# A transformer layer's W_out and W_up stages: splits held to the end of the DFT, products begun in parts, combinations spread over steps

## The chip, the core and the metric

The kernel runs on one core of a Trainium2 chip. Its engines work side by side, each with its own instruction queue that is taken in order: TensorE (PE in the profile; PEld is its weight load) multiplies matrices into PSUM banks, VectorE (DVE), ScalarE (ACT) and GpSimd (POOL) work element by element, SyncE (SP) issues most DMAs. An instruction that waits for data holds up everything behind it in its own queue. The metric is device microseconds of one execution; the time of a kernel is the median of its runs.

## What is computed

One layer of a bidirectional encoder and a last norm, for two groups of tokens with shared weights: the "sample" (512 tokens) and the "prompt" (1024 tokens), with 16 meta tokens ahead of each. All data is float32, D is 1024, the hidden width 4096.

```python
def encoder_layer(x, w_in, rel_bias, meta_bias, w_branch_na, w_branch_fn, w_out, g_mix, g_mlp, w_up, w_down):
    h = rmsnorm(x, g_mix)
    z = h @ w_in
    q, k, v, u, gate_na, gate_fn = jnp.split(
...
    y_na = neighbourhood_attention(q, k, v, rel_bias, meta_bias).reshape(B, N, NA_WIDTH) @ w_branch_na
    y_fn = fourier_mix(u) @ w_branch_fn
    mixed = jax.nn.sigmoid(gate_na) * y_na + jax.nn.sigmoid(gate_fn) * y_fn
    x = x + mixed @ w_out
    a = jax.nn.relu(rmsnorm(x, g_mlp) @ w_up)
    return x + (a * a) @ w_down
```

`fourier_mix` is the real part of a 2-D DFT over positions and channels.

## The kernel before

**Float32 by splits.** A product of float32 matrices is made of three fast ones: each operand is split into a rounded part `hi` and a rest `lo`, and `mm3` issues hi·hi, hi·lo and lo·hi into one PSUM bank. For a weight tile a DMA on SP loads `w_raw` (L145), ScalarE casts it to `w_hi` (L151), and GpSimd subtracts to get `w_lo` (L152). The buffers `w_raw`, `w_hi` and `w_lo` of `wtile` exist twice each; tiles can be given other places.

**The order.** The sample goes through all stages first, then the prompt. In each: attention, gates, the merge of the attention branch, the Fourier stage (`fourier_channels` for the channels, split into `uc` and `us` at L132 and L133; `fourier_positions`, the DFT over positions, which leaves `fs` and splits it into `fT` at L982 to L997), `merge_fn` (W_fn, eight tiles `dm`), `project_out` (W_out), W_up, W_down. The program is written in this order, but the framework's scheduler orders each engine's queue by its own estimate of when operands are ready, so an instruction written later can stand ahead of one written earlier. Two helpers bound that freedom: `behind(marks)` puts what is issued inside it behind the marked instructions in the queues of the engines that the marks belong to (it adds no wait for them to end), and `pinned()` does so with the last instruction written so far on every engine, TensorE included.

**W_out's weights** are eight pieces of 256 rows by 512 columns; the generator `out_weights` makes one load and split per `next(wout)`. `merge_fn` asks for one after every second tile, so four in all (L891); the other four are asked for after it. The pieces' places differ: in the sample, the first lies in the MLP pool's `w` pair, four in `wo` pairs, one in `wu`, one in the `hi`/`lo` buffers of `wtile`, the last in the `w` pair again.

**The merge.** In `merge_fn` VectorE multiplies each product with its gate (L884) and adds the attention branch (L885); for each pair of tiles ScalarE casts the sum (L889) and VectorE subtracts (L890). The result `m` has four parts, each of them two of the eight blocks that W_out's products sum over. During the sample's Fourier stage VectorE also combines W_fn's columns for both groups (`fn_ahead`, L801 to L809).

**W_out's products.** For the sample (`Layer.project_out`) a half of the columns at a time, for four tiles of 128 tokens, each a bank of 24 products, added to the residual `acc` (L1025). In the second half each token tile is then normed, transposed on TensorE (L193) and split into `h2T`, two tiles behind. Then the first two W_up tiles begin with the first 256 tokens (`up`, step 256; L1065 to L1070), and the last two transposes stand between. `Mlp.run` then goes on with these tiles' second half, and with the next tiles in steps of 512; after every second pair come the products with W_down (`down`).

For the prompt (`Halves.project_out`) the order of token tiles and halves is written out by hand in `steps`, with two kinds of banks in turn, and `flush` puts transposes where they are due.

**W_up for the prompt** (`Halves.up`) works in sixteen groups `g` of two tiles. It is a Strassen-like scheme: seven products of twelve matmuls each instead of eight, from combined weights that `prepare` makes for the next group (GpSimd at L1305, ScalarE at L1308), one step of it behind each product. VectorE adds the products (L1416, L1423, L1426), the relu's squares follow (L1433), and four combinations of them (L1439) are made for the W_down stage, in two tiles `h0` and `h1` that are stored by DMA (L1441).

Of the kernel before, what the change touches and what calls it, by code (L numbers as in the profile page):

```python
# [22 lines left out]
ALU = mybir.AluOpType  # L23
# [45 lines left out]
class Layer:  # L69
# [783 lines left out]
    def merge_fn(self, br, mp, T, fT, mixed, sig, gate, wout, marks):  # L853

        nc = self.nc
        m = []
        ready, self.fn_ready = self.fn_ready, []
        got, banks = {}, {}
# [14 lines left out]
        for dm in range(8):  # L873
            if dm % 2 == 0:
                total = []
            total.append(mp.tile([128, D], F32, name="hn", bufs=2)[:, :T])
            sg, mx = (t[dm // 2][:, dm % 2] for t in (sig, mixed))
            for c in range(T // 512):
                cs = slice(c * 512, (c + 1) * 512)
                if (dm, c) in banks:  # L880
                    py = product(dm, c, self.LAST[-1:], banks[dm, c], more=True)
                else:
                    py = product(dm, c, self.LAST, self.psum())
                nc.vector.tensor_tensor(out=sg[:, cs], in0=py, in1=sg[:, cs], op=ALU.mult)  # L884
                nc.vector.tensor_tensor(out=total[-1][:, cs], in0=mx[:, cs], in1=sg[:, cs], op=ALU.add)  # L885
            if dm % 2:
                m.append((gate(), gate()))
                for i in range(2):
                    nc.scalar.copy(out=m[-1][0][:, i], in_=total[i])  # L889
                    nc.vector.tensor_tensor(out=m[-1][1][:, i], in0=total[i], in1=m[-1][0][:, i].bitcast(F32), op=ALU.subtract)  # L890
                self.wo.append(next(wout))  # L891
        return m
# [65 lines left out]
    def fourier_positions(self, q, fp, name, T, u, cos, sin):  # L958
        nc = self.nc
# [7 lines left out]
        for m in self.LAST:  # L967
            fs = q.tile([128, K], F32, name="fs", bufs=2)
            for k0, kn in kchunks:
                ps = self.psum()  # L970
                ops = []
# [22 lines left out]
            else:  # L994
# [3 lines left out]
                                               op0=ALU.mult, op1=ALU.subtract)  # L998
        return fT, marks

# [7 lines left out]
    def project_out(self, hp, p, x, T, m, wo, acc, mlp, marks):  # L1008
# [5 lines left out]
        for t in range(nt):  # L1014
            nc.sync.dma_start(acc[t], x[t * 128:(t + 1) * 128, :])
        pending = []
        for half in range(2):
            cs = slice(half * 512, (half + 1) * 512)
            w = wo[4 * half:4 * half + 4]
            for t in range(nt):  # L1020
                ts = slice(t * 128, (t + 1) * 128)
# [119 lines left out]
class Halves:  # L1141
# [55 lines left out]
    def project_out(self, hp, mp, m, wo):  # L1197
# [12 lines left out]
        def flush(n):  # L1210
            with layer.behind(layer.mark((mybir.EngineType.PE,))):
                for x in due.pop(n, ()):
                    self.turn(*x)

        def product(n, t, half):
# [3 lines left out]
            ps = layer.psum(("mm", "o")[n % 2])  # L1219
            layer.mm3(ps, [(m[kt // 2][0][:, kt % 2, ts], m[kt // 2][1][:, kt % 2, ts], w[kt // 2][0][:, kt % 2], w[kt // 2][1][:, kt % 2])  # L1220
                           for kt in range(8)])
            nc.vector.tensor_tensor(out=acc[t][:, cs], in0=acc[t][:, cs], in1=ps, op=ALU.add)
# [169 lines left out]
    def up(self, mp):  # L1392

        layer, nc, TH = self.layer, self.nc, self.TH
        for g in range(self.NF // 2):
            steps = self.prepare(g + 1)

            def step():
                with layer.pinned():
                    next(steps, None)  # L1400

# [30 lines left out]
            for i, x in enumerate((r, r_)):  # L1432
                nc.vector.tensor_tensor(out=x, in0=x, in1=x, op=ALU.mult)  # L1433
                nc.sync.dma_start(to[:, i * 2 * TH:(i + 1) * 2 * TH], x)
            h = [self.tile(f"h{i}") for i in range(2)]
            s1, s2, s3, s4 = (x[:, y] for x in h for y in (left, right))
            for k, x, y, op in ((s1, r[:, right], r_[:, right], ALU.add), (s2, s1, r[:, left], ALU.subtract),
                                (s3, r[:, left], r[:, right], ALU.subtract), (s4, r_[:, left], s2, ALU.subtract)):
                nc.vector.tensor_tensor(out=k, in0=x, in1=y, op=op)  # L1439
# [205 lines left out]
```

## Time and profile before

| | us |
|---|---|
| median of 3 runs | 2032.23 |
| lowest, highest | 2029.92, 2033.35 |
| the profiled execution | 2034.05 |
| its span, first to last instruction | 2032.3 |

The page of the profile counts, for each engine, the busy time, its share of the span and the instructions. A row of the timeline has the start in us from the span's start, the duration, the engine, the line of the kernel, the operation, output<-inputs and shapes; in brackets stands how long the engine was idle before it and what released it. A row that ends in x2 or more holds several instructions in a row. In the table by stretch, each engine's busy time and number of instructions come first, in the order PE, PEld, DVE, ACT, POOL, then the granted TensorE clock as a share of full speed, the DMA engines' busy share and GB/s.

### The profile page before, as it was taken

How to read it: one execution, taken by the hardware profiler on the slowest of the kernel's cores; microseconds unless marked ns; L12 is line 12 of the kernel's file. 1: busy time of each engine (PE TensorE's matmuls, PEld its weight loads, DVE VectorE, ACT ScalarE, POOL GpSimd, SP SyncE). 2: the span in 40 equal slices, each digit the busy share in tenths (PEclk: the TensorE clock that was granted, in tenths of full speed). 3: DMA queues.
4: the chain of work that ended last, by engine and by line, in shares of the span. 5: the costliest groups of instructions: out<-in, count | busy, mean ns of one | idle time of the engine just before them, and what ended most of it. 6: DMA issues, size and time to landing. Idle time of an engine off the chain costs nothing.

```text
span 2032.3 us, 26413 instructions
## 1 busy us (share of the span) xinstructions
PE 1955.3 (96%) x9611; PEld 1622.2 (80%) x9611; DVE 1138.2 (56%) x1914; ACT 756.4 (37%) x1323; POOL 961.9 (47%) x743
## 2 busy tenths in 40 slices
PE   6999979999999989999999999999999999999997
PEld 4887767888888878888888888787787888888886
DVE  6672434666665552566663226566767776442246
ACT  3564322433333221556552313124333333533342
POOL 3244535366777641233333226113788785544442
PEclk9999989999999999999999999999999999999999
DMA  6666772344444445455455544222445445976663
GB/s 204 170 160 213 213 219 83 121 138 158 155 145 154 148 149 207 116 140 139 136 179 167 142 111 146 99 72 77 169 150 196 157 154 180 312 238 201 196 190 122
DMA packets 275652, 326.50 MB, mean 161 GB/s; under 512 B 42872, under 2 KB 197240, under 8 KB 274968
## 3 DMA queue, kind: packets, MB, share of 16 engines
q1 hardware_dynamic: 261792, 303.92, 46.9%
q0 software_dynamic: 13728, 20.88, 4.4%
q8 instruction: 76, 1.25, 0.3%
q14 instruction: 56, 0.46, 0.1%
HBM read 235.67 MB, written 91.64 MB: 161 GB/s over the span
## 4 chain that ended last, share of the span: by engine, by line
PE 77%; DVE 7%; DMA 5%; issue 4%; POOL 4%; ACT 3%; SPq 0%; POOLq 0%; DVEq 0%; ACTq 0%
PE ps_mm L128 22%; PE ps_o L128 20%; PE ps_s L128 17%; PE ps_t L128 7%; PE ps_mm L487 2%; PE ps_mm L488 2%; PE ps_mm L489 2%; PE ps_o L629 1%; POOL w_lo L152 1%; DVE hn L885 1%; PE ps_t L609 1%; DVE gate L890 1%; DMA w_raw<-in_w_in 1%; DMA gain<-in_w_fnB 1%; DMA w_raw<-in_w_out 1%
## 5 line engine op out<-in xcount | busy, mean ns | idle before, releaser
L152 POOL TENSOR_TENSOR w_lo<-w_raw,w_hi 128x1024 fp32r<-128x1024 f32 x84 | 212.4, 2537 | 228.1 <-ACT w_hi L151 202.8
L151 ACT CAST w_hi<-w_raw 128x1024 fp32r<-128x1024 f32 x100 | 104.8, 1049 | 168.5 <-PE ps_mm L128 49.9
L1068 DVE TENSOR_TENSOR relu<-relu 128x512 f32<-128x512 f32 (+1 forms) x34 | 65.6, 1929 | 109.2 <-ACT relu L1067 109.0
L487 PE MATMUL ps_mm<-hT,w_hi 128*128 128x512 f32 (+3 forms) x320 | 125.9, 393 | 0.0
L488 PE MATMUL ps_mm<-hT,w_hi 128*128 128x512 f32 (+3 forms) x320 | 114.8, 359 | 0.0
L489 PE MATMUL ps_mm<-hT,w_lo 128*128 128x512 f32 (+3 forms) x320 | 114.7, 358 | 0.0
L1305 POOL TENSOR_TENSOR x<-w_hi,x 128x512 fp32r<-128x512 f32 (+1 forms) x42 | 78.6, 1872 | 22.8 <-ACT x L1308 22.8
L603 ACT ACTIVATE sc<-sc,ast 128x288 f32<-128x288 f32 (+4 forms) x96 | 53.9, 562 | 78.4 <-DVE ast L601 78.0
L152 POOL TENSOR_TENSOR w_lo<-r,w_hi 128x1024 fp32r<-128x1024 f32 x15 | 35.9, 2395 | 96.7 <-ACT w_hi L151 96.7
L723 POOL MEMSET bm<- 64x96 f32 (+2 forms) x64 | 11.2, 176 | 144.3 <-DVE ast L601 105.5
L629 PEld LDWEIGHTS ps_o<-pt,vb 104*64 104x64 f32 (+6 forms) x576 | 61.7, 162 | 11.7 <-POOL vb L566 5.0
L152 POOL TENSOR_TENSOR w_lo<-w_hi 128x1024 fp32r<-128x1024 f32 x18 | 47.1, 2615 | 48.7 <-ACT w_hi L151 48.7
L128 PE MATMUL ps_t<-gate,x 128*128 128x512 f32 x264 | 65.5, 397 | 2.7 <-DVE r_lo L1416 2.7
L152 POOL TENSOR_TENSOR w_lo<-w_lo,w_hi 128x1024 fp32r<-128x1024 f32 x18 | 45.9, 2551 | 45.6 <-ACT w_hi L151 45.6
L489 PEld LDWEIGHTS ps_mm<-hT,w_lo 128*128 128x128 f32 x320 | 60.1, 188 | 8.5
L629 PE MATMUL ps_o<-pt,vb 104*64 104x128 f32 (+6 forms) x576 | 62.8, 244 | 4.0 <-POOL vb L566 2.3
L566 POOL TENSOR_TENSOR vb<-vr,vb 96x384 fp32r<-96x384 f32 (+4 forms) x48 | 48.6, 1032 | 35.5 <-ACT vb L565 30.2
L128 PE MATMUL ps_mm<-gate,x 128*128 128x512 f32 x256 | 64.2, 395 | 0.0
L488 PEld LDWEIGHTS ps_mm<-hT,w_hi 128*128 128x128 f32 x320 | 60.7, 190 | 1.7
L487 PEld LDWEIGHTS ps_mm<-hT,w_hi 128*128 128x128 f32 x320 | 60.6, 189 | 1.7
L128 PEld LDWEIGHTS ps_t<-gate,x 128*128 128x128 f32 x264 | 48.7, 188 | 16.1 <-DVE r_lo L1416 5.1
L601 DVE CUSTOM_DVE_ANT_0 sc<-ps_s,bm 128x288 f32<-128x288 f32 (+4 forms) x96 | 46.3, 482 | 26.9 <-PE ps_s L597 10.9
(672 smaller groups left out, 5890.3 us busy)
## 6 DMA issues: line engine op xcount, KB each, us to landing
w_raw<-in_w_in SPq DMA_DIRECT2D x56, 512.0 KB
w_raw<-in_w_up SPq DMA_DIRECT2D x34, 512.0 KB
wt<-hn SPq DMA_DIRECT2D x32, 512.0 KB
hidden_prompt<-h SPq DMA_DIRECT2D x32, 512.0 KB
w_hi<-hidden_prompt SPq DMA_DIRECT2D x20, 512.0 KB
w_raw<-hidden_prompt SPq DMA_DIRECT2D x18, 512.0 KB
w_lo<-hidden_prompt SPq DMA_DIRECT2D x18, 512.0 KB
w_raw<-in_w_out SPq DMA_DIRECT2D x16, 512.0 KB
```

Source lines behind the costliest of these rows:

```text
L128: self.nc.tensor.matmul(out, a, b, start=(i == 0 and not more), stop=(i == len(terms) - 1), skip_group_check=more)
L151: nc.scalar.copy(out=hi, in_=raw)
L152: (lo_engine or nc.gpsimd).tensor_tensor(out=lo, in0=raw, in1=hi.bitcast(F32), op=ALU.subtract)
L487: nc.tensor.matmul(ps, a[0], b[0], start=(kt == 0), stop=False)
L488: nc.tensor.matmul(ps, a[0], b[1], start=False, stop=False)
L489: nc.tensor.matmul(ps, a[1], b[0], start=False, stop=(kt == 7))
L566: nc.gpsimd.tensor_tensor(out=lo, in0=vs, in1=hi.bitcast(F32), op=ALU.subtract)
L601: nc.vector.tensor_tensor_reduce(out=sc[:, :W], in0=ps[:, :W], in1=bm[:, :W], scale=1.0, scalar=3e38, op0=ALU.add, op1=ALU.min, accum_out= ...
L603: nc.scalar.activation(out=sc[:, :W], in_=sc[:, :W], func=AF.Exp, bias=st[:, 0:1], scale=-1.0, accum_out=st[:, 1:2])
L629: nc.tensor.matmul(po[:m, j * 128:(j + 1) * 128], v, x, start=(i == 0), stop=(i == len(ops) - 1))
L1068: nc.vector.tensor_tensor(out=r, in0=r, in1=r, op=ALU.mult)
L1305: self.nc.gpsimd.tensor_tensor(out=to, in0=x, in1=y, op=op)
```

## The change

It has five parts.

- `fourier_positions` also returns a mark of the last ScalarE and the last GpSimd instruction written in it, and `merge_fn` asks for its four W_out pieces behind these marks: the casts and subtractions of W_out may no longer be queued ahead of the DFT's own on these two engines. SP's queue is not marked.
- Sample, `project_out`: the first two banks get their products over the first six of eight blocks, one bank after the other, before either gets its last two blocks. The number of products is the same.
- Prompt, `Halves.project_out`: the same for its first two steps.
- Sample: the third W_up tile is loaded into the MLP pool's `w` pair instead of the `wtile` buffers, is worked in steps of 256 tokens, and its first half is issued ahead of `Mlp.run`.
- Prompt, `Halves.up`: the four combinations and their two stores leave the end of their group; a generator issues them one by one in the steps of the next group, behind its products. Those of the last group follow the loop.

```diff
     merge_fn
+        marks, split = marks
...
-                self.wo.append(next(wout))
+                with self.behind(split):
+                    self.wo.append(next(wout))
     fourier_positions
-        return fT, marks
+        return fT, (marks, self.mark((mybir.EngineType.Activation, mybir.EngineType.Pool)))
     project_out (sample)
+        def product(ps, half, t, blocks, more=False):
+            ts = slice(t * 128, (t + 1) * 128)
+            w = wo[4 * half:4 * half + 4]
+            self.mm3(ps, [(m[kt // 2][0][:, kt % 2, ts], m[kt // 2][1][:, kt % 2, ts], w[kt // 2][0][:, kt % 2], w[kt // 2][1][:, kt % 2])
+                          for kt in blocks], more=more)
+            return ps
+        banks = {(0, t): product(self.psum(), 0, t, range(6)) for t in range(2)}
         for half in range(2):
...
-                ps = self.psum()
-                self.mm3(ps, [(m[kt // 2][0][:, kt % 2, ts], m[kt // 2][1][:, kt % 2, ts], w[kt // 2][0][:, kt % 2], w[kt // 2][1][:, kt % 2])
-                              for kt in range(8)])
+                if (half, t) in banks:
+                    ps = product(banks[half, t], half, t, range(6, 8), True)
+                else:
+                    ps = product(self.psum(), half, t, range(8))
...
         mlp.load(1)
-        for f in range(2):
+        mlp.load(2, self.pair(p, [128, 2, 512], "w", 2))
+        for f in range(3):
             next(mlp.ups[f])
-            self.transpose_in(*pending.pop(0))
+            if pending:
+                self.transpose_in(*pending.pop(0))
     Mlp
-    def load(self, f):
+    def load(self, f, to=None):
         if f not in self.w:
-            self.w[f] = self.layer.weights(self.layer.rows("w_up", f * 128))
+            to = to and [x.rearrange("p a (k c) -> p (a k) c", c=128) for x in to]
+            self.w[f] = self.layer.weights(self.layer.rows("w_up", f * 128), to)
...
-            step = 256 if f < 2 and T == 512 else 512
+            step = 256 if f < 3 and T == 512 else 512
     Halves.project_out (prompt)
+            if n < 2 and n not in banks:
+                banks[n] = layer.psum(("mm", "o")[n % 2])
+                layer.mm3(banks[n], ops[:6])
+                return
+            ps = banks[n] if n < 2 else layer.psum(("mm", "o")[n % 2])
+            layer.mm3(ps, ops[6 if n < 2 else 0:], more=n < 2)
...
+        for n in range(2):
+            product(n, *steps[n])
     Halves.up (prompt)
+        combining = iter(())
...
                 with layer.pinned():
+                    next(combining, None)
                     next(steps, None)
...
-            h = [self.tile(f"h{i}") for i in range(2)]
-            s1, s2, s3, s4 = (x[:, y] for x in h for y in (left, right))
-            for k, x, y, op in ((s1, r[:, right], r_[:, right], ALU.add), (s2, s1, r[:, left], ALU.subtract),
-                                (s3, r[:, left], r[:, right], ALU.subtract), (s4, r_[:, left], s2, ALU.subtract)):
-                nc.vector.tensor_tensor(out=k, in0=x, in1=y, op=op)
-            for i, x in enumerate(h, 2):
-                nc.sync.dma_start(to[:, i * 2 * TH:(i + 1) * 2 * TH], x)
+            combining = self.combinations(r, r_, to)
+        for _ in combining:
+            pass
+    def combinations(self, r, r_, to):
+        yield
+        h = [self.tile(f"h{i}") for i in range(2)]
+        s1, s2, s3, s4 = (x[:, y] for x in h for y in (left, right))
+        for i, (k, x, y, op) in enumerate(((s1, r[:, right], r_[:, right], ALU.add), (s2, s1, r[:, left], ALU.subtract),
+                                           (s3, r[:, left], r[:, right], ALU.subtract), (s4, r_[:, left], s2, ALU.subtract))):
+            nc.vector.tensor_tensor(out=k, in0=x, in1=y, op=op)
+            if i % 2:
+                nc.sync.dma_start(to[:, (i // 2 + 2) * 2 * TH:(i // 2 + 3) * 2 * TH], h[i // 2])
+            yield
```

More of the change, by code (lines that the diff above doesn't have):

```diff
@@ L1016, in project_out @@
         pending = []
+        def product(ps, half, t, blocks, more=False):
[5 more added lines that the diff above has]
+        banks = {(0, t): product(self.psum(), 0, t, range(6)) for t in range(2)}
         for half in range(2):
             cs = slice(half * 512, (half + 1) * 512)
-            w = wo[4 * half:4 * half + 4]
             for t in range(nt):
-                ts = slice(t * 128, (t + 1) * 128)
-                ps = self.psum()
-                self.mm3(ps, [(m[kt // 2][0][:, kt % 2, ts], m[kt // 2][1][:, kt % 2, ts], w[kt // 2][0][:, kt % 2], w[kt // 2][1][:, kt % 2])
-                              for kt in range(8)])
+                if (half, t) in banks:
+                    ps = product(banks[half, t], half, t, range(6, 8), True)
+                else:
+                    ps = product(self.psum(), half, t, range(8))
                 nc.vector.tensor_tensor(out=acc[t][:, cs], in0=acc[t][:, cs], in1=ps, op=ALU.add)
@@ L1213, in flush @@
                     self.turn(*x)
+        banks = {}
         def product(n, t, half):
@@ L1218, in product @@
             w = wo[4 * half:4 * half + 4]
-            ps = layer.psum(("mm", "o")[n % 2])
-            layer.mm3(ps, [(m[kt // 2][0][:, kt % 2, ts], m[kt // 2][1][:, kt % 2, ts], w[kt // 2][0][:, kt % 2], w[kt // 2][1][:, kt % 2])
-                           for kt in range(8)])
+            ops = [(m[kt // 2][0][:, kt % 2, ts], m[kt // 2][1][:, kt % 2, ts], w[kt // 2][0][:, kt % 2], w[kt // 2][1][:, kt % 2])
+                   for kt in range(8)]
+            if n < 2 and n not in banks:
[4 more added lines that the diff above has]
+            layer.mm3(ps, ops[6 if n < 2 else 0:], more=n < 2)
             nc.vector.tensor_tensor(out=acc[t][:, cs], in0=acc[t][:, cs], in1=ps, op=ALU.add)
@@ L1434, in up @@
                 nc.sync.dma_start(to[:, i * 2 * TH:(i + 1) * 2 * TH], x)
-            h = [self.tile(f"h{i}") for i in range(2)]
-            s1, s2, s3, s4 = (x[:, y] for x in h for y in (left, right))
-            for k, x, y, op in ((s1, r[:, right], r_[:, right], ALU.add), (s2, s1, r[:, left], ALU.subtract),
-                                (s3, r[:, left], r[:, right], ALU.subtract), (s4, r_[:, left], s2, ALU.subtract)):
-                nc.vector.tensor_tensor(out=k, in0=x, in1=y, op=op)
-            for i, x in enumerate(h, 2):
-                nc.sync.dma_start(to[:, i * 2 * TH:(i + 1) * 2 * TH], x)
+            combining = self.combinations(r, r_, to)
+        for _ in combining:
+            pass
+    def combinations(self, r, r_, to):
+        nc, TH = self.nc, self.TH
+        left, right = slice(0, TH), slice(TH, 2 * TH)
+        yield
[7 more added lines that the diff above has]
+            yield
     DOWN = ((0, "b11", 0), (5, "t2", 1), (2, "b21", 0), (6, "t3", 1), (4, "t1", 0), (3, "t4", 1), (7, "b22", 0))
```

## The prediction, made before the change was run

> **What bounds the kernel now.** The page comes first: it says which engine fills the span.
>
> ```profile
> span 2032.3 us, 26413 instructions
> PE 1955.3 (96%) x9611; PEld 1622.2 (80%) x9611; DVE 1138.2 (56%) x1914; ACT 756.4 (37%) x1323; POOL 961.9 (47%) x743
> ```
>
> TensorE is busy 96% of the span and the change alters no product, so it can win only from the 77 us in which TensorE stands still and from stretches at a lower clock. The second view is the list of TensorE's waits, asked for the sample's stages from the DFT to W_up (285 to 400 us), then for the prompt's (1222 to 1440 us). These rows stand where the change touches code:
>
> ```profile
> PE ps_s L128 <- ACT us L132: 9.3, 1, 9.3
> PE ps_mm L128 <- ACT gate L132: 2.3, 1, 2.3
> PE ps_o L128 <- ACT gate L889: 1.9, 1, 1.9
> ...
> PE ps_t L128 <- DVE r_lo L1416: 2.7, 1, 2.7
> PE ps_o L128 <- POOL w_lo L152: 1.9, 1, 1.9
> PE ps_mm L128 <- POOL fT L989: 1.3, 1, 1.3
> PE ps_mm L128 <- ACT gate L889: 0.9, 1, 0.9
> ```
>
> Columns: who waited for whom, total us, times, longest. Each is a single wait, so each can be looked up in the timeline. The third view, busy time by stretch, has the granted clock third from the right:
>
> ```profile
> 292.00:299.00 7.00, 0.09 (x1) 0.09 (x1) 0.10 (x1) 1.44 (x3) 0.32 (x1) 0.50 0.83 262
> 384.00:391.00 7.00, 6.59 (x25) 5.71 (x26) 5.31 (x6) 2.33 (x5) 6.92 (x5) 0.51 0.24 74
> 1268.00:1271.00 3.00, 3.00 (x8) 2.32 (x8) 3.00 (x2) 1.57 (x2) 2.71 (x2) 0.51 0.20 68
> 1440.00:1754.00 314.00, 314.00 (x1353) 252.75 (x1352) 224.24 (x172) 108.52 (x156) 241.76 (x143) 1.00 0.52 180
> ```
>
> Three of the waits are followed by a half clock; after the one at 384 us it lasts nearly 7 us of full work. And from 1440 to 1754 us, the prompt's W_up steps, TensorE never stands still: whatever the change does there can only keep or lose.
>
> **Part 1, W_out's splits behind the DFT, sample.** In time order, engine by engine:
>
> ```profile
> 297.56 1.04 ACT L151 CAST w_hi<-w_raw 128x1024 fp32r<-128x1024 f32 x1 [15.93 <-DMA w_raw<-in_w_out]
> 298.51 0.35 ACT L132 CAST us<-ps_s 7x252 fp32r<-7x252 f32 x1
> ...
> 286.76 0.53 PE L128 MATMUL ps_s<-w_hi,us 128*128 128x266 f32 x3
> 289.23 0.39 PE L128 MATMUL ps_s<-w_hi,us 128*128 128x266 f32 x1 [1.95 <-DVE us L133]
> 298.92 1.03 PE L128 MATMUL ps_s<-w_hi,us 128*128 128x266 f32 x2 [9.30 <-ACT us L132]
> ...
> 290.40 0.76 DVE L801 TENSOR_TENSOR raw<-raw,gain 128x256 f32<-128x256 f32 x2 [1.22 <-DMA gain<-in_w_fnB]
> 298.89 0.41 DVE L133 TENSOR_TENSOR us<-ps_s,us 7x252 fp32r<-7x252 f32 x1 [7.73 <-ACT us L132]
> ...
> 292.11 0.91 SPq L145 DMA_DIRECT2D w_raw<-in_w_out  x2
> ```
>
> ScalarE stood for 15.93 us at the first W_out cast, whose data was asked for only at 292.11; behind it waited the 0.35 us cast of seven rows of `us` that the DFT needs. The change puts that W_out cast behind the DFT's last ScalarE instruction. What is late next is the VectorE half of the same split: if it keeps its place behind the weight combinations (L801, done at 291.16) it ends at about 291.6 instead of 299.3. From there the order is the same, so the DFT and the merge behind it start 7.3 to 7.7 us earlier; I take 7.3. Bounds: the whole wait, 9.3, plus about 1.5 us if the half clock of 292 to 302 us (3.1 us of it under work) also goes, so 10.8; and 5.0, if one of the costs below appears.
>
> The clock: TensorE stays nearly idle from 287.3 to 291.6 us even then, about as long as it took to drop before (287.3 to about 291.9). I leave that half clock in. The Trainium skill, TensorE: Matmul & The Clock Gate, Part 1: The HAM clock gate, says the clock is halved after an idle window of about 3.4 us and given back after as long a busy one. By that rule the sum is the same here, and the drop at 292 agrees; but the drop at 384 followed a wait of 2.25 us only. By the rule's letter part 4 below would win the wait alone, some 2.7 instead of 4.2, and the sum would be 2016.5; the measured 0.51 decides.
>
> What the move delays: the W_out casts, their subtractions on GpSimd, and the DMAs of later pieces, which wait for a raw buffer to come free. W_out's DMAs go past nothing on SP: the marks are on ScalarE and GpSimd.
>
> ```profile
> 298.68 2.39 POOL L152 TENSOR_TENSOR w_lo<-w_raw,w_hi 128x1024 fp32r<-128x1024 f32 x1 [17.44 <-ACT w_hi L151]
> ...
> 313.87 0.40 PE L128 MATMUL ps_s<-fT,w_hi 128*128 128x512 f32 x1
> ...
> 325.11 0.40 PE L128 MATMUL ps_o<-w_hi,gate 128*128 128x512 f32 x1
> ```
>
> With the DFT over at about 296.5, pieces 0 and 1 are split by 302.2 (2.39 each on GpSimd), pieces 2 and 3, whose DMAs wait for these two, by about 309 to 312. W_out's first product comes at 325.11 - 7.3 = 317.8. That cover of some 6 us hides the move. A tighter one: the fifth W_fn tile's product, 313.87 before, comes at 306.6, and if a W_out cast that waits for its DMA (about 304) stands ahead of that tile's cast, TensorE waits up to 2.3 us. That gives the 5.0.
>
> **Part 2, the same edit in the prompt.**
>
> ```profile
> 1242.53 2.60 POOL L152 TENSOR_TENSOR hid_lo<-w_raw,hid_hi 128x1024 fp32r<-128x1024 f32 x1
> 1245.09 1.70 POOL L989 TENSOR_TENSOR fT<-fs,fT 128x505 fp32r<-128x505 f32 x1
> ...
> 1261.34 2.94 POOL L152 TENSOR_TENSOR w_lo<-w_raw,w_hi 128x1024 fp32r<-128x1024 f32 x1 [0.44 <-ACT w_hi L151]
> 1264.24 2.25 POOL L152 TENSOR_TENSOR w_lo<-raw,w_hi 128x512 fp32r<-128x512 f32 x1
> ```
>
> The two first rows change places, and the 1.33 us wait for `fT` goes. But GpSimd is occupied almost without a gap until 1266.5, where TensorE waits 1.94 us for a W_fn piece that stands behind six W_out pieces. Arriving 1.4 us sooner, it waits 1.4 us longer. So 0. Bounds: minus 2.5 (GpSimd another 0.6 us late, since the next W_out DMA is issued 1.7 us later, and a longer half clock), plus 5 (the last W_out piece falls behind the W_fn piece: 1.3 + 1.9 and the 1.6 us lost at half clock).
>
> **Part 3, W_out's first products in two parts.** Sample: the wait at 329.96.
>
> ```profile
> 329.96 0.50 PE L128 MATMUL ps_o<-wo_hi,gate 128*128 128x512 f32 x1 [1.90 <-ACT gate L889]
> ...
> 329.94 1.29 DVE L890 TENSOR_TENSOR gate<-hn,gate 128x512 fp32r<-128x512 f32 x2 [0.68 <-ACT gate L889]
> ```
>
> The same 24 products per bank are issued, 18 of two banks first: 36 by 0.23 us (the row of 394.65 in part 4 has 16 in 3.7 us) are 8.4 us from 325.11, to 333.5, while the late `m` is split by 331.2. The wait goes with its slow first product: 2.0. In the prompt the 0.88 us wait goes in the same way: 1.0. Each is at least half of that unless `m` comes over 2 us later.
>
> **Part 4, the third W_up tile by token halves (sample).**
>
> ```profile
> 381.15 0.60 PE L193 MATMUL ps_t<-ident,hn 128*128 128x128 f32 x4
> 384.00 0.58 PE L128 MATMUL ps_mm<-gate,w_hi 128*128 128x256 f32 x1 [2.25 <-ACT gate L132]
> 391.50 1.10 PE L128 MATMUL ps_mm<-gate,w_lo 128*128 128x256 f32 x8
> ...
> 394.65 3.82 PE L128 MATMUL ps_o<-gate,w_hi 128*128 128x512 f32 x16
> ...
> 382.09 1.04 ACT L151 CAST w_hi<-r 128x1024 fp32r<-128x1024 f32 x1 [1.79 <-DMA r<-in_w_down]
> ...
> 388.28 1.27 DVE L133 TENSOR_TENSOR gate<-ps_t,gate 128x256 fp32r<-128x256 f32 x3
> ```
>
> (The row of 391.50 is followed at 392.44: eight products in 0.94 us.) Between 381.75 and 394.65 stand 48 products of 256 columns at 0.118, four of 512 at 0.234 and four transposes: 7.1 us of work in 12.9. So 5.8 are lost, the 2.25 us wait and mostly the half clock. The added half tile gives 24 products, 2.8 us, that need only the first 256 tokens. They reach from 381.75 to 384.6, past the release at 384.0. The last transposes' copies end only at 389.55, about 0.7 us after what can then run (half tile and the first four of eight blocks of two tiles, 6.6 us, and transposes). I take 4.2, leaving 1.6 for this and for four small relu steps more on ScalarE and VectorE. Bounds 0 and 5.8. The third tile's weights lie elsewhere (the buffers of W_out's first piece, free at 349), so they are early; in exchange the second W_down tile must wait for the third W_up tile's second half, about 393, and is split by 397, two or three us before the down products at about 399.
>
> **Part 5, combinations spread over W_up (prompt).**
>
> ```profile
> 1428.16 2.77 DVE L1439 TENSOR_TENSOR h<-r_hi,r_lo 128x512 f32<-128x512 f32 x1
> ...
> 1434.26 0.67 DVE L1416 TENSOR_TENSOR r_lo<-r_hi,ps_s 128x512 f32<-128x512 f32 x1
> ...
> 1436.57 3.06 PE L128 MATMUL ps_t<-gate,x 128*128 128x512 f32 x12 [2.66 <-DVE r_lo L1416]
> ```
>
> In the first of the sixteen groups the combinations (L1439) stand ahead of the next group's three additions (L1416), and TensorE waits 2.66 us once. Later groups run at the delay this left, without waiting. Spread, one combination stands behind each addition. I take 2.7; bounds 0 and 2.8. The hidden stores (two DMAs a group) move with them; nothing reads them before the down stage.
>
> **Sum.** 7.3 + 0 + 2.0 + 1.0 + 4.2 + 2.7 = 17.2 us. The profiled execution took 2034.05 us (1.75 outside the span), so 2016.9; it lies 1.8 above the median of the runs shown, 2032.23, so **2015.0**.
>
> **The rivals.** *More is won*: VectorE's `us` is taken before L801 and the half clock at 292 does not come (+3.5), and the prompt's W_fn piece goes first (up to +5): about 2008. For it: both orders are open once the cast is gone. Against: L801 stands in front now. Chance 0.14. *Part is given back*: the W_fn cast waits behind a W_out cast (-2.3) and part 4's gain is lost to the W_down tile or a half clock (-4.2): 2021.5. For it: GpSimd is occupied in both places. Chance 0.19. *The change doesn't do what it says*: some other DMA-bound cast still precedes `us` on ScalarE (the W_fn casts are candidates), the 7.3 go, and with part 4 gone too 2026.5 to 2029. Against: only the W_out cast lies in that gap. Chance 0.06. *Slower*: the combinations now stand between additions that TensorE needs. Beside GpSimd one takes 0.69 to 2.77 us:
>
> ```profile
> L1439 DVE TENSOR_TENSOR h<-r_hi,r_lo x16: 692/2764/2771, 1428.2 to 1720.2; 128x512 f32<-128x512 f32 x16
> ```
>
> Three additions of 0.69 and two combinations must fit into three products of 2.8 us, 8.4. That holds up to 3.17 us for one; beyond, each of 15 groups loses twice the excess. To eat 17.2 and 4 more, one would have to take 3.9: about 2037. Chance 0.03. The Trainium skill, SBUF — State Buffer, Who interferes with whom, speaks against this part: a VectorE instruction with two SBUF inputs and a GpSimd one that reads SBUF block each other fully. The 2764 against 692 ns agree; by that rule one could wait for a whole 2.5 us instruction of GpSimd and take 3.2, which would cost some 1 us in all.
>
> **How the numbers follow.** Forecast 0.58, between 2010 and 2020. The range of 2007 to 2025 takes in the first rival and the second and most of the bounds, and leaves out the other two and tails. About 0.2% (4 us) is what a measurement of this kernel can tell from no change: faster by more 0.91 (the forecast and the first two rivals), within it 0.06 (the third, whose times straddle the bound), slower 0.03.
>
> **What would show it.** Right: no ScalarE wait for W_out between 282 and 297 us and TensorE's `us` wait under 3 us; no wait at W_out's first product; full clock where 384 to 391 was; no wait in the second W_up group. The prediction falls if TensorE waits for a W_fn or W_out `lo` in the merges, for W_down's second tile, or between 1440 and 1754 us.

## The result

| kernel | runs | median, us | lowest, highest |
|---|---|---|---|
| before | 4 | 2031.08 | 2028.85, 2033.35 |
| changed | 4 | 2016.12 | 2014.89, 2016.88 |

The ratio is 0.9926, 95% interval 0.9909 to 0.9943: the change wins 15.0 us. In a second, later set (the run e9_after below) it was 0.9921 (0.9907 to 0.9935). The forecast was 2015.0.

### The profile page after: what moved, and what is told of

The parts are those of the page before. It is cut to its first block, busy times and chain, and to the rows that moved or that the text cites. A ratio compares the mean times of both kernels' runs of the same rounds, so it can differ in the third digit from the quotient of the medians.

```text
span 2013.1 us, 26468 instructions
## 1 busy us (share of the span) xinstructions
PE 1950.7 (97%) x9635; PEld 1621.2 (81%) x9635; DVE 1105.3 (55%) x1916; ACT 757.2 (38%) x1325; POOL 958.9 (48%) x743
## 4 chain that ended last, share of the span: by engine, by line
PE 80%; DMA 6%; DVE 5%; issue 3%; POOL 3%; ACT 2%; SPq 1%; POOLq 0%; ACTq 0%; DVEq 0%
PE ps_mm L128 21%; PE ps_o L128 20%; PE ps_s L128 18%; PE ps_t L128 8%; PE ps_mm L487 2%; PE ps_mm L488 2%; PE ps_mm L489 2%; POOL w_lo L152 2%; PE ps_o L629 1%; DMA w_raw<-in_w_in 1%; DMA w_raw<-in_w_out 1%; PE ps_t L609 1%; DMA gain<-in_w_fnB 1%; PE ps_t L193 1%; DMA sin<-in_sin_prompt 1%
## 5 line engine op out<-in xcount | busy, mean ns | idle before, releaser
L1330 POOL TENSOR_TENSOR x<-w_hi,x 128x512 fp32r<-128x512 f32 (+1 forms) x42 | 66.2, 1576 | 23.8 <-ACT x L1333 23.8
```

The costliest lines, as they stand in the source:

```text
L1330: self.nc.gpsimd.tensor_tensor(out=to, in0=x, in1=y, op=op)
```

## The profile after

First the page of the changed kernel, the line of its span and that of the engines:

```profile
span 2013.1 us, 26468 instructions
PE 1950.7 (97%) x9635; PEld 1621.2 (81%) x9635; DVE 1105.3 (55%) x1916; ACT 757.2 (38%) x1325; POOL 958.9 (48%) x743
```

TensorE is busy 4.6 us less than before and stands still 14.6 us less: 62.4 us of the span in place of 77.0. The list of its waits (who waited for whom, total us, times, longest) in the sample's stages, 280 to 400 us, and in the prompt's, 1210 to 1450 us, says which stalls went and which came:

```profile
PE ps_s L128 <- DVE us L133: 3.1, 2, 1.5
PE ps_t L193 <- DVE gate L133: 1.5, 2, 1.3
PE ps_s L128 <- POOL w_lo L152: 0.9, 1, 0.9
...
PE ps_mm L128 <- POOL w_lo L152: 2.7, 1, 2.7
PE ps_s L128 <- POOL w_lo L152: 2.0, 2, 1.2
PE ps_mm L128 <- DMA sin<-in_sin_prompt: 1.4, 1, 1.4
```

Gone are the 9.3 us for ScalarE's `us`, both waits for the last `m` at W_out, the 2.3 us of the third W_up tile, the 1.3 us for `fT` and the 2.7 us for the addition in W_up. New are a wait for a W_fn `lo` in the sample (0.9), one ahead of the last transposes (1.5), and longer ones for W_fn in the prompt. The 1.4 us for the DMA of `sin` does not belong to the change: waits of 0.4 to 1.3 us for it stand in five other traces, among them e12 (0.9), which leaves the prompt's DFT and merge as they were. The timeline shows each in its place:

```profile
288.27 0.76 DVE L801 TENSOR_TENSOR raw<-raw,gain 128x256 f32<-128x256 f32 x2 [0.97 <-DMA gain<-in_w_fnB]
288.94 0.40 DVE L133 TENSOR_TENSOR us<-ps_s,us 7x252 fp32r<-7x252 f32 x1
289.40 0.39 PE L128 MATMUL ps_s<-w_hi,us 128*128 128x266 f32 x1 [1.53 <-DVE us L133]
292.07 0.63 PE L128 MATMUL ps_mm<-fT,w_hi 128*128 128x512 f32 x1
295.57 1.05 ACT L151 CAST w_hi<-w_raw 128x1024 fp32r<-128x1024 f32 x1 [2.40 <-DMA w_raw<-in_w_out]
...
372.69 0.63 PE L193 MATMUL ps_t<-ident,hn 128*128 128x128 f32 x4 [1.34 <-DVE gate L133]
382.14 2.08 PE L128 MATMUL ps_mm<-gate,w_hi 128*128 128x256 f32 x16
...
1243.52 1.71 POOL L152 TENSOR_TENSOR w_lo<-raw,w_hi 128x512 fp32r<-128x512 f32 x1
1245.28 0.50 PE L128 MATMUL ps_s<-fT,w_lo 128*128 128x512 f32 x1 [1.21 <-POOL w_lo L152]
1253.72 0.79 PE L128 MATMUL ps_mm<-fT,w_lo 128*128 128x512 f32 x1 [2.70 <-POOL w_lo L152]
```

ScalarE's W_out cast (295.57) now waits for its DMA where nobody waits for ScalarE. What ends TensorE's wait before the DFT is VectorE's half of the `us` split, right behind the combinations of L801, as forecast. Busy time by stretch (the clock is third from the right):

```profile
292.00:294.00 2.00, 2.00 (x7) 1.61 (x6) 0.85 (x2) 0.78 (x2) 1.26 (x2) 0.50 0.87 212
384.00:388.00 4.00, 4.00 (x24) 3.47 (x24) 2.87 (x2) 1.49 (x4) 2.24 (x2) 1.00 0.45 126
1253.70:1256.70 3.00, 2.98 (x7) 2.40 (x8) 3.00 (x3) 1.57 (x2) 2.80 (x2) 0.50 0.64 196
1440.00:1740.00 300.00, 300.00 (x1294) 242.49 (x1292) 179.11 (x162) 106.69 (x152) 225.25 (x135) 1.00 0.53 186
```

The half clock at 292 stayed, the one at 384 went, and W_up runs without a gap as before.

The two profiled executions differ by 19.2 us, 4.2 more than the medians. About 2 of it stand in code that is the same in both, ahead of the DFT. These are the waits between 170 and 250 us, first of the kernel before, then of the second profile of the changed kernel (e9_after, 2021.93 us):

```profile
PE ps_s L128 <- POOL w_lo L152: 2.2, 1, 2.2
```

```profile
PE ps_s L128 <- POOL w_lo L152: 2.5, 1, 2.5
```

The first profile of the changed kernel has no such wait. It comes and goes from one execution to the next.

## The experiments

Three sets on three chips, each beside the kernel before on its own chip. "Gained" is one minus the ratio, times 2032 us; its interval is about 2.5 us to each side (2 for the runs with one part alone), so a difference of two entries is uncertain by about 3.

| run | what it is | median | ratio (95%) | gained |
|---|---|---|---|---|
| e1_no_hold | without part 1 and 2 | 2024.27 | 0.9958 (0.9946 to 0.9970) | 8.5 |
| e2_no_parts | without part 3 | 2022.67 | 0.9950 (0.9938 to 0.9962) | 10.2 |
| e3_no_third | without part 4 | 2019.35 | 0.9934 (0.9922 to 0.9945) | 13.4 |
| e4_no_spread | without part 5 | 2021.26 | 0.9943 (0.9931 to 0.9955) | 11.6 |
| e5_hold_sample | without part 2 | 2015.99 | 0.9933 (0.9919 to 0.9946) | 13.6 |
| e6_rest_late | all, and W_out's last four pieces later | 2012.95 | 0.9914 (0.9900 to 0.9927) | 17.5 |
| e7_comb_late | all, and the last combinations later | 2014.17 | 0.9920 (0.9906 to 0.9933) | 16.3 |
| e8_all | e5, e6 and e7 together | 2008.69 | 0.9892 (0.9879 to 0.9906) | 21.9 |
| e9_after | the changed kernel again | 2017.02 | 0.9921 (0.9907 to 0.9935) | 16.1 |
| e10_only_hold | before with parts 1 and 2 alone | 2030.46 | 0.9987 (0.9978 to 0.9997) | 2.6 |
| e11_only_parts | before with part 3 alone | 2030.18 | 0.9989 (0.9980 to 0.9999) | 2.2 |
| e12_only_third | before with part 4 alone | 2030.79 | 0.9993 (0.9984 to 1.0002) | 1.4 |

The changed kernel's two sets give 15.0 and 16.1; 15.5 is used below.

### Each part taken out of the changed kernel

**The hold.**

```diff
     merge_fn
-                with self.behind(split):
-                    self.wo.append(next(wout))
+                self.wo.append(next(wout))
```

> The changed kernel with W_out's splits no longer held behind the DFT, in both groups of tokens. My theory (the parts add up, each at its own place): ScalarE's 9.3 us wait comes back and TensorE's wait for the seven rows of us with it; the sample loses 7.6 (what the trace of the changed kernel gained between 277 us and the first W_fn product), the prompt regains some 1.5 (its 1.33 us wait returns, the 2.7 us wait for a W_fn piece shrinks); so 6 us more than the changed kernel, about 2022, or 0.4 to 0.5% faster than the kernel before. Rival A (the two microseconds that the changed kernel already led by before the DFT belong to this part too): 9.6 lost and 1.5 regained, 2024. Rival B (the later parts hide what the DFT loses, since W_out is then split long before its products): 3 or less lost, 2019.

Seven us are lost (15.5 - 8.5); the median, 2024.27, lies at rival A and within the noise of the theory. The wait is back, and longer than before:

```profile
PE ps_s L128 <- ACT us L132: 10.1, 1, 10.1
```

Rival B falls: what the DFT loses isn't hidden later. Part 1's mechanism is shown.

**The two parts of W_out's products.**

```diff
     project_out (sample)
-        banks = {(0, t): product(self.psum(), 0, t, range(6)) for t in range(2)}
+        banks = {}
     Halves.project_out (prompt)
-            if n < 2 and n not in banks:
-                banks[n] = layer.psum(("mm", "o")[n % 2])
-                layer.mm3(banks[n], ops[:6])
-                return
-            ps = banks[n] if n < 2 else layer.psum(("mm", "o")[n % 2])
-            layer.mm3(ps, ops[6 if n < 2 else 0:], more=n < 2)
+            ps = layer.psum(("mm", "o")[n % 2])
+            layer.mm3(ps, ops)
...
-        for n in range(2):
-            product(n, *steps[n])
```

> The changed kernel with W_out's first two products again whole, in both groups. My theory: each group waits once more for the last pair of m at its first product, sample 1.9 with a slow product behind it, prompt 0.9: 3 us more, 2019. Rival (by position the trace of the changed kernel gained only about 1 us between the merge and W_out's second bank, because a wait of 0.85 us for a W_fn lo stands in the same stretch and stays): 1 to 2 us more, and in the trace the sample's wait under 1 us.

Neither: 5.3 us are lost. The waits and the stretch behind tell why:

```profile
PE ps_o L128 <- ACT gate L890: 3.4, 1, 3.4
```

```profile
324.00:330.00 6.00, 6.00 (x16) 4.65 (x16) 1.55 (x3) 1.95 (x3) 4.72 (x2) 0.55 0.22 55
```

The sample's wait for the last `m` is 3.4 us here, against 1.9 in the kernel before, and now a half clock follows: 16 products in 6 us, where the six us behind them hold 27. In the kernel before the 1.9 us wait was followed by full clock. So with the hold in place, part 3 is worth about 5.

**The third W_up tile.**

```diff
     project_out (sample)
-        mlp.load(2, self.pair(p, [128, 2, 512], "w", 2))
-        for f in range(3):
+        for f in range(2):
     Mlp.up
-            step = 256 if f < 3 and T == 512 else 512
+            step = 256 if f < 2 and T == 512 else 512
```

> The changed kernel with the third W_up tile again in the weight buffers, worked whole, behind the first two. My theory: the 2.25 us wait for the last transposes' split returns and the half clock behind it, for 6 to 7 us; 4 to 5 us more, 2020 to 2021. Rival (the half clock of the kernel before at 384 to 391 us was not caused by this wait): the wait alone, some 2.3 us, 2018, with full clock behind it.

Two us are lost by the ratio, as the rival said; the median, 2019.35, lies between the rival's 2018 and the theory's 2020. But the trace has what the theory says, the wait with a half clock behind it, though not quite the old one: a wait of 1.6, one of 1.1 for a W_down tile, then the clock at 0.60 for 4 us:

```profile
PE ps_mm L128 <- ACT gate L132: 1.6, 1, 1.6
PE ps_s L128 <- POOL w_lo L152: 1.1, 1, 1.1
```

```profile
376.00:380.00 4.00, 4.00 (x18) 3.19 (x18) 3.48 (x6) 1.43 (x4) 3.92 (x3) 0.60 0.08 27
```

So this run doesn't settle the size; the traces of all runs, set side by side at e12 below, do.

**The spread combinations.**

```diff
     Halves.up
-            combining = self.combinations(r, r_, to)
+            for _ in self.combinations(r, r_, to):
+                pass
```

> The changed kernel with the four combinations of a group made at the group's end again. My theory: one wait of 2.7 us in front of the second group of the prompt's W_up and none later, 2.7 us more, 2019. Rival A: the wait is taken up by the slack of later groups, no difference, 2016. Rival B (spread combinations cost time by standing between additions, so that undoing them wins): less than 2016.

3.9 us are lost in the median, whose runs scatter from 2018.50 to 2024.10. The trace has one wait between 1400 and 1460 us, and none later in W_up:

```profile
PE ps_t L128 <- DVE r_lo L1443: 2.6, 1, 2.6
```

Set against the changed kernel's, this trace is 0.15 us ahead shortly before that place, 2.7 behind after it, and 2.7 to 2.8 behind through all later groups. The theory stands, both rivals fall. The other traces agree: over the first groups of the prompt's W_up the nine with part 5 gain 2.9 us on the kernel before, the four others without it less than 0.05.

### One part alone

The four losses are 7.0, 5.3, 2.1 and 3.9, together 18.3 against a whole of 15.5, a surplus that is within the noise of four such differences. The waits say more: taking out one part also uncovers what another one had covered. So three parts were put alone into the kernel before, by the edits above the other way round.

> The changed kernel once more, beside the three that follow, so that one part alone can be set against all five on the same chip: 15 us under the kernel before, 2016, give or take 2.

> The kernel before with nothing but the hold of W_out's splits behind the DFT. Theory (the parts are tied: with the hold one W_out split more runs on GpSimd beside the sample's merge, VectorE's two-input instructions there take up to 2.2 us instead of 1.1, the last m comes later against W_out's first product): the DFT ends 7.6 to 9.6 earlier, but that product then waits 3.4 instead of 1.9 us with a half clock behind it, so 3 to 4 us are given back; 4 to 5 less than before, about 2026.5. Rival (the parts add): 7.5 less, 2023.5, with a wait of 1.9 us.

> The kernel before with nothing but W_out's first products in two parts, in both groups. Theory (tied, as in the run before this one): without the hold there is only the wait of 1.9 us and that of 0.9 us to win, 3 less than before, 2028. Rival (the parts add, and this one is worth the 5 to 6 us that undoing it cost): 2025.5.

> The kernel before with nothing but the third W_up tile by token halves. Theory (its own place, tied to no other part): the wait of 2.25 us and the half clock behind it go, 4 less, 2027. Rival (what undoing it cost in the median is all of it): 2 to 3 less, 2028.5.

The hold alone wins 2.6, less even than the theory of tied parts said. In its trace the first `us` wait is as short as in the changed kernel, but at W_out's first product stands the wait that e2 had, with the half clock behind it (waits from 280 to 340 us, and a stretch):

```profile
PE ps_o L128 <- ACT gate L890: 3.4, 1, 3.4
```

```profile
325.00:328.00 3.00, 3.00 (x9) 2.32 (x8) 0.00 (x0) 0.00 (x0) 3.00 (x2) 0.50 0.07 8
```

Followed along VectorE's instructions, this kernel leads the one before (does the same instruction earlier) by 9.3 us at the first eviction of the sample's merge, where VectorE first reads a bank of it (2 to 3 of it from the wait at 200 us), by 7.7 at the last but one pair of `m`, and by 5.0 at the first eviction of W_out: 4.3 are given back, 2.7 of them at W_out's first product. Where the `m` falls behind can be read from one instruction of VectorE, in the kernel before and in this one:

```profile
318.92 1.06 DVE L885 TENSOR_TENSOR hn<-gate 128x512 f32<-128x512 f32 x1
```

```profile
310.12 2.17 DVE L886 TENSOR_TENSOR hn<-gate 128x512 f32<-128x512 f32 x1
```

It is the same addition (one line further in the file). With the hold, the splits of W_out on GpSimd fall beside other instructions of the merge, and from the first eviction to the last subtraction VectorE takes 24.1 us (298.47 to 322.56) instead of 22.2 (307.74 to 329.94). TensorE then stands 3.4 instead of 1.9 us. That GpSimd is the cause of the longer addition is argued from the rows, not tried by itself. The rows are clear, though: GpSimd works without a gap from 296.24 to 313.44 us, and VectorE's seven instructions with two inputs in SBUF that start in that time take 1.01 to 2.90 us, the nine behind it 0.68 or 0.69; those that read a PSUM bank take 0.68 or 0.69 throughout.

Part 3 alone wins 2.2: the 1.9 and the 0.9 us waits, nothing else, as the theory had it. So hold and parts are worth 2.6 and 2.2 one by one, while taking either out of the whole costs 7.0 or 5.3. The intervals of these are too wide to prove a tie, but the 3.4 us wait, there in e2 and e10, absent with both parts and 1.9 with neither, shows it. So does the lead over the kernel before, followed in every trace from the merge's last subtraction to W_out's second eviction in the sample: it falls by 2.6 us with the hold but without part 3 (e2, e10), grows by 1.8 to 2.2 with part 3 but without the hold (e1, e11) and by 3.7 in all eight with both, and stays as it is in e12, which has neither.

The third tile alone wins 1.4 (-0.4 to 3.3), less than its theory. The old wait went, but the new one, ahead of the last transposes, is here followed by a half clock (timeline, and the stretch behind):

```profile
383.07 0.63 PE L193 MATMUL ps_t<-ident,hn 128*128 128x128 f32 x4 [1.55 <-DVE gate L133]
```

```profile
384.00:390.00 6.00, 5.79 (x37) 5.76 (x37) 3.89 (x10) 2.32 (x7) 0.00 (x0) 0.72 0.30 90
```

In the profiled execution of the changed kernel the same wait, 1.34 us, was not. All traces together give the size. From W_out's last eviction to the third one of W_down in the sample, the lead over the kernel before grows by 3.9 to 4.5 us in six of the ten traces with part 4, and by 2.6 to 2.7 in the other four, where a half clock of 3.4 us follows this wait; in the three others without part 4 it grows by 0.1 to 0.5.

### What was left in the merges

**The hold in the sample only.**

```diff
-                with self.behind(split):
+                with self.behind(split if T == 512 else []):
```

> The changed kernel with the hold only in the sample; in the prompt W_out's splits may again stand ahead of the DFT's. Theory (GpSimd is full in the prompt's merge, and the hold puts two splits more in front of a W_fn piece): the waits of 1.21 and 2.70 us for W_fn's lo shrink by more than the 1.33 us wait for fT costs; 1.5 us less than the changed kernel, about 2014.6. Rival (the order behind the DFT doesn't matter, GpSimd's total sets it): no difference, 2016, the wait for fT back and the others shorter by as much.

Undecided: 13.6 gained against 15.5 can't tell the theory's 1.5 us from the rival's nothing. The waits of the merge show the exchange, 1.3 for `fT`, and 2.5 for W_fn's pieces instead of the 4.7 with the hold, so 3.8 against 4.7, a gain of 0.9 that lies between the two:

```profile
PE ps_mm L128 <- POOL w_lo L152: 1.9, 1, 1.9
PE ps_s L128 <- POOL fT L992: 1.3, 1, 1.3
PE ps_s L128 <- POOL w_lo L152: 0.6, 1, 0.6
```

**W_out's last four pieces behind W_fn's last split (prompt).**

```diff
     merge_fn
                     got[dm] = raw if isinstance(raw, tuple) else self.fn_weights(br, dm, raw)
+                    self.fn_last = self.mark((mybir.EngineType.Activation, mybir.EngineType.Pool))
     the layer, prompt
-                with self.behind(self.mark()):
+                with self.behind(self.mark() + self.fn_last):
                     rest = list(wout)
```

> The changed kernel with the prompt's last four W_out pieces held behind W_fn's last split on ScalarE and GpSimd. Theory (W_fn's small splits wait behind W_out's large ones on GpSimd, and the W_out pieces are not needed before about 1302 us): the waits of 2.70 and 0.76 us go, and the half clock of 1253 to 1257 us with them (some 1.4); 4 to 5 us less, about 2011.5. Rival A (the W_fn pieces wait for their own DMA): little changes, 2015 to 2016. Rival B (the W_out pieces then come late): W_out's second half waits, slower than 2016 by up to 3.

The interval reaches from 15 to 20 us gained, so the median alone (2012.95 against 2016.12 and 2017.02) doesn't prove it; the trace does for the place: the 2.7 us wait and the half clock behind it are gone, one of 1.1 is left, and no wait for a W_out piece came.

**The last combinations behind the DFT (sample).**

```diff
     fourier_channels
-                    for _ in range(2 - part):
+                    for _ in range(2 - 2 * part):
     the layer, behind fourier_positions
+            with self.pinned(): list(ahead)
```

> The changed kernel with the last two W_fn combinations of the sample behind the DFT instead of between VectorE's three us splits. Theory (VectorE waits there for the DMAs of W_fn, and the us splits behind it): TensorE's two waits of 1.5 us for us go, and the half clock from 292 to 294 us (1 us) with them; 3 to 4 us less, 2012.5. Rival A: the combinations now delay the first merge products' evictions and W_fn pieces 6 and 7: 0 to 1 us less. Rival B: the half clock stays, 3 less.

VectorE now takes the three `us` splits in a row, and TensorE runs through the DFT without a wait at full clock:

```profile
282.51 0.41 DVE L133 TENSOR_TENSOR us<-ps_o,us 128x252 fp32r<-128x252 f32 x1
282.84 0.41 DVE L133 TENSOR_TENSOR us<-ps_mm,us 128x252 fp32r<-128x252 f32 x1
283.17 0.40 DVE L133 TENSOR_TENSOR us<-ps_s,us 7x252 fp32r<-7x252 f32 x1
```

```profile
285.00:288.00 3.00, 3.00 (x20) 2.73 (x20) 1.93 (x5) 1.57 (x4) 1.42 (x2) 1.00 1.01 330
```

The split of the seven rows comes 5.8 us earlier than in the changed kernel's profile, 1.6 of them from ahead of the DFT. Of these 3.1 are left at the first eviction of the merge, 5.4 to 5.6 from its last subtraction to the end of W_out, and 3.7 behind the last transposes, which are followed by a half clock here. Rival B falls, since the half clock at 292 is gone. The medians differ by 2 to 3, between the theory and rival A, and their intervals exclude neither.

**All three.**

> The three edits of the runs before this one together. If they act at their own places they add: 1.5 + 4.5 + 3.5, less what the first two share (both shorten the same waits on GpSimd, so 5 for these two): about 2007.5. If the first two are one and the same gain, and the third is taken up by the W_fn pieces of the sample: about 2011.

2008.69, the fastest of all: 21.9 us under the kernel before, and its interval (0.9879 to 0.9906) lies below both of the changed kernel's. The expected sum, 2007.5, is nearly reached, though the other forecast, 2011, lies within the interval too. In the prompt's merge these waits are left:

```profile
PE ps_s L128 <- POOL fT L992: 1.3, 1, 1.3
PE ps_mm L128 <- DVE gate L891: 0.5, 1, 0.5
```

## Why the prediction was right, and where it wasn't

The forecast was a sum of 17.2 us, and 15.0 came (15.5 over both sets). The mechanism of every part was the one named; three sizes were off (parts 1, 3 and 4), and the sum hides that two of its terms are not independent.

- **Part 1, 7.3.** Right up to the start of the merge. At the first eviction of the merge the changed kernel leads by 9.6 us in the profiles, 2.0 of them from ahead of the DFT: 7.6. VectorE stayed behind L801 and the half clock at 292 stayed, both as said. The named danger came too: a W_fn tile's split waits behind W_out's on GpSimd, for 0.85 us, where up to 2.3 was allowed. What was not seen is what the hold does behind that point. "From there the order is the same" doesn't hold: the merge gives part of the gain back, in the changed kernel's profile from a lead of 9.6 us to 6.9 at its last subtraction. Alone the hold then loses another 2.7 us at W_out's first product (e10).
- **Part 2, 0.** Not contradicted: e5 can't tell the hold in the prompt from none. The wait for `fT` went and the W_fn piece waits longer, as said, but by 2.2 us in all, not by 1.4. From the prompt's DFT to the end of its merge the lead falls by 2.2 us in the changed kernel's first profile, which has the `sin` wait and a half clock there, and by 0.2 in its second.
- **Part 3, 2.0 and 1.0.** The step that failed is "the wait goes with its slow first product: 2.0". It took the wait from the kernel before, 1.9, for a kernel in which the merge comes 7 us earlier. There it would be 3.4 with a half clock (e2). In the sum this costs nothing: what part 3 covers more, part 1 would have lost without it. The pair was put at 9.3 for the sample; the lead grew from 2.0 to 9.9 us by the end of W_out, so 7.9. The prompt's 1.0 came as 1.2, from a lead of 12.8 us at the end of the merge to 14.0 at W_out's second bank.
- **Part 4, 4.2.** Right in the profiled execution, where the lead grows from 9.9 at the end of W_out to 14.4 at the third eviction of W_down, 4.5; high on average, since the ten traces with part 4 show 2.6 to 4.5, and the medians 2.1 (taken out) and 1.4 (alone), each with a wide interval. The 1.6 left "for this and for four small relu steps" is the 1.5 us wait ahead of the last transposes. But the sum took the full clock behind it as given, and in e12 it wasn't. The rule weighed there (the Trainium skill, TensorE: Matmul & The Clock Gate, Part 1: The HAM clock gate), that only an idle window of about 3.4 us halves the clock, gave 2.7; its result is near the median, though its reason isn't borne out, since a half clock does follow waits of 1.6 us (e3, e12).
- **Part 5, 2.7.** Right: 2.9 in the profiles, 2.7 in e4's trace. VectorE has room: one combination takes 0.68 to 2.28 us in the changed kernel, far from the 3.17 at which the slower rival would begin.
- **The profile against the median.** 1.8 us were taken off. A likely cause of the slow profile can be seen, the 2.2 us wait at 200 us, which other executions do not have.
- **What was to show it.** No wait at W_out's first product, full clock where 384 to 391 was, no wait in the second W_up group: all three came. "No ScalarE wait for W_out between 282 and 297 us" was drawn too wide: there is one of 2.4, ending at 295.57, which holds up nobody, and TensorE's two waits for `us` make 3.1 instead of under 3. Of what would make the sum fall, the waits for W_fn's `lo` in the merges did come, 0.9 in the sample and 4.7 in the prompt, against 2.5 in the prompt before; they cost a microsecond or two, not the sum.
- **The rivals.** *More is won* asked for VectorE's `us` ahead of L801 and W_fn's piece ahead in the prompt, 2008 together. The change does neither; e8 does both by other edits and has 2008.69. *Part is given back* came in small: 0.85 us at the W_fn tile, and part 4's half clock in some executions. *Doesn't do what it says* and *slower* are out.

## What to carry to other kernels

Price two edits on neighbouring stages as a pair: a stage that is moved earlier brings its own lateness to the next product, and an edit that covers a small wait today may be what makes the first one pay (2.6 and 2.2 us alone, 7.0 and 5.3 when taken out). An instruction that waits for a DMA on an in-order engine should stand behind all that the next products need; when one such place is cleared, look at the other engine that serves the same products (here VectorE's combinations, then GpSimd's splits), because the wait moves there in shortened form. And don't price a stall of two us by what one profile shows behind it.

## What the runs showed of the hardware

I had not expected that the clock after one and the same wait differs from execution to execution. Ahead of the prompt's W_up stands a wait of 3.6 us in code that the change doesn't touch. Timeline and stretch of the kernel before:

```profile
1392.11 1.08 PE L1192 MATMUL ps_s<-ident,h 128*128 128x128 f32 x4 [3.55 <-DVE gate L133]
```

```profile
1392.00:1395.00 3.00, 2.89 (x13) 2.76 (x14) 1.87 (x6) 1.66 (x6) 1.27 (x1) 0.50 0.51 142
```

And of the changed kernel:

```profile
1378.08 0.63 PE L1207 MATMUL ps_s<-ident,h 128*128 128x128 f32 x4 [3.57 <-DVE gate L133]
```

```profile
1378.00:1381.00 3.00, 2.89 (x17) 2.15 (x17) 2.81 (x9) 2.73 (x9) 1.27 (x1) 1.00 0.47 136
```

The same four transposes take 1.08 us in one and 0.63 in the other. The code ahead of them is not the cause: in the second profile of the changed kernel (e9_after) they take 1.09 again, behind the same wait.

```profile
1383.14 1.09 PE L1207 MATMUL ps_s<-ident,h 128*128 128x128 f32 x4 [3.55 <-DVE gate L133]
```

In the same way the 2.70 us wait at 1253.72 of the changed kernel has 7 products in the 3 us behind it, at 0.50, and the wait of 2.57 at the same place of e4_no_spread has 13:

```profile
1252.60:1255.60 3.00, 2.99 (x13) 2.50 (x14) 3.00 (x3) 1.57 (x2) 2.79 (x2) 1.00 0.60 193
```

Take all TensorE waits of 0.8 us or more between 180 and 1460 us in the fourteen traces, where the clock had been full. A clock under 0.9 within the next 3 us followed 18 of 67 waits below 1.5 us (many of these with another wait close by), about two thirds of some 75 from 1.5 to 2.8 us, and 18 of 20 longer ones. The half clock lasts 3.4 us or a multiple of that, mostly 3.4 or 6.8, and costs about 1.4 us of products in 3 us. The Trainium skill, TensorE: Matmul & The Clock Gate, Part 1: The HAM clock gate, says that the window in which activity is measured runs freely and does not start with the kernel. That fits these rows. That it takes a whole idle window of about 3.4 us does not fit, since waits of 1.5 to 2.8 us are followed by a half clock more often than not.

The traces show what decides. In each of them the granted clock changes only on a grid of 3.41 us, which lies differently from trace to trace. Take the stretches of this grid from 100 to 1990 us that have full clock. Where TensorE was busy for less than 0.44 of a stretch, the next one had a half clock in 49 of 50 cases; at 0.56 or more in none of 7543; in between in 22 of 48. So it matters how much of one stretch a wait empties, not how long the wait is. The wait of 3.57 us in the changed kernel's first profile falls on two stretches, busy for 1.75 and 1.50 of 3.41 us, and the clock stays; in its second profile the same wait leaves 0.93 us of one stretch, and the clock drops:

```profile
1372.77:1376.18 3.41, 1.75 (x16) 1.51 (x14) 3.23 (x10) 1.60 (x5) 0.00 (x0) 1.00 1.21 307
1376.18:1379.60 3.42, 1.50 (x12) 1.29 (x12) 3.14 (x12) 3.31 (x9) 0.71 (x1) 1.00 0.88 256
```

```profile
1378.66:1382.08 3.42, 0.93 (x9) 0.69 (x7) 3.35 (x9) 2.10 (x5) 0.00 (x0) 1.00 1.17 318
1382.08:1385.49 3.41, 2.35 (x11) 2.38 (x12) 2.29 (x8) 2.54 (x9) 1.27 (x1) 0.50 0.67 186
```

With some ten such waits in each execution, this can make a spread of several us; waits that come and go, like the one of 2.5 us at 200 us, add to it (2014.21 to 2021.93 for the changed kernel in one set). A gain of 1 to 3 us can't be told from it by a single profile.
